# Sliding-window attention in a hybrid decoder layer: one logit per key column, and value sums over block differences

## The chip, the cores and the metric

The kernel runs on one core of a Trainium2 chip. The metric is the device time of one execution in microseconds. The kernel before took 890.16 us (median of three runs, 889.65 to 890.69).

## What is computed

One decoder layer on 512 tokens of width 1024. A shared RMS-normalised input feeds two branches: a chunkwise mLSTM with 4 heads, and sliding-window attention with 16 query heads of width 64, 4 key/value heads and one sink logit per head. The branches are gated, merged and projected, and an MLP, a gated per-layer embedding and a final norm follow. The change lies in the attention alone:

```python
W = SW_WINDOW            # 128, so 4 blocks of queries
kb, vb = band(k), band(v)        # a block's keys: left neighbour's 128, then its own 128
logits = einsum("bnqhgd,bnkhd->bnhgqk", qb, kb) * SW_HEAD_DIM ** -0.5
diff = qi + W - ki
band_mask = (diff >= 0) & (diff < W)
logits = where(valid, logits, -inf)              # block 0 has no left neighbour
m = maximum(max(logits, -1), sink)
pexp = exp(logits - m)
probs = pexp / (sum(pexp, -1) + exp(sink - m))
out = einsum("bnhgqk,bnkhd->bnqhgd", probs, vb)
```

For query row q of a block and column k from 0 to 127, the mask lets through the block's own key k if k <= q, and the left neighbour's key k if k > q. So of the two keys in column k exactly one is valid.

## The kernel before

The layer is one program of five in-order instruction streams (TensorE, VectorE, ScalarE, GpSimd, SyncE), and the framework orders the instructions of each stream from the Python code. Weights arrive in fp32, and nearly every projection is made of three matmuls per product: `split` (L134) lets ScalarE round a tile to a high part (L137, `wh`) and VectorE subtract for the low part (L138, `wl`), and `chain` (L171) multiplies high by high, high by low and low by high. One projection of 512 columns is a chain of 24 matmuls into an accumulator `psg`, of which there are two.

PSUM is shared out in three tags: two `psg` and two `pst` tiles of 128x512, and two `psa` tiles of 128x1024. The attention takes its logits and its transposes from the two `psa` tiles, and the value sums from `pst`.

The attention works in units (kp, n, ab): a pair of key heads, a block n of 128 queries and one key head of the pair, with four query heads `g` each; 16 units in all, 12 of them with n > 0. Two functions carry it.

- `swa_probs` (L683): eight score matmuls (L689 with the high part of the keys, L690 with the low part) fill a `psa` tile with 4 x 256 logits. VectorE's custom instruction (L697, four per unit, 256 columns or 128 for n = 0) scales, adds the mask `band` and takes the row maximum with the sink into `mx`, writing the logits to `lm`. After two small VectorE steps (L701, L703), ScalarE takes four exponentials with row sums (L708), and VectorE normalises (L709, L711, L712).
- `swa_out` (L715), once per pair of units: for each of the two key blocks (`nk`, one for n = 0), TensorE transposes eight 128x128 pieces of `lm` into a `psa` tile (L726) and ScalarE copies it to `pT` (L728). Two matmuls in fp32 per block (L734, two records each in the trace) then sum the values `vs` into a `pst` tile, which four `split` steps turn into `yb`.

The loop (L750) scores two units ahead (`LOOK`) and puts one query or mLSTM projection (`q_proj`, `qk_proj`) between units as filling for TensorE. The masks are built once at the start: `band` on GpSimd (L213 to L216), and `tri` (L217), which is 0 where column >= row and -1e30 elsewhere. At the start GpSimd also rounds the first weights (L327), VectorE subtracts for their low part (L328) and for that of the normalised input (L317).

Of the kernel before, what the change touches and what calls it, by code (L numbers as in the profile page):

```python
# [22 lines left out]
NEG = -1e30  # L23
# [13 lines left out]
def block_kernel(  # L37
# [30 lines left out]
    V, A, G, T = nc.vector, nc.scalar, nc.gpsimd, nc.tensor  # L68
# [12 lines left out]
    c1 = pool(st_s, "c1", side="right")  # L81
    sp = pool(st_s, "sp", side="right")
# [4 lines left out]
    def nm(s):  # L87
        n_names[0] += 1
        return f"{s}_{n_names[0]}"
# [8 lines left out]
    def ps_a():  # L98
        return pp.tile([P, 1024], F32, tag="a", bufs=2, name=nm("psa"))
# [23 lines left out]
    def tok_scratch(n="lm"):  # L123
        return sp.tile([P, D], F32, tag="lm", bufs=LMB, name=nm(n))
# [9 lines left out]
    def split(dst, src, scale=None):  # L134

        if scale is None:
            A.copy(dst[0], src)  # L137
            last_low[0] = V.tensor_sub(dst[1], src, r32(dst[0]))  # L138
        else:
            A.activation(dst[0], src, AF.Copy, scale=scale)  # L140
            V.scalar_tensor_tensor(dst[1], src, scale, r32(dst[0]), ALU.mult, ALU.subtract)
# [60 lines left out]
    ident = cp.tile([P, P], F32, name="ident")  # L202
# [4 lines left out]

    cp.tile([P, 16], F32, name="pad")
    V.memset(eps_t, EPS)
    zeros4 = c1.tile([4, P], F32, name="zeros4")  # L210
    V.memset(zeros4, 0.0)
    band = c1.tile([P, 2 * P], F32, name="band")
    G.memset(band, 0.0)  # L213

    G.affine_select(out=band, in_=band, pattern=[[1, 2 * P]], compare_op=ALU.is_gt, fill=NEG, base=0, channel_multiplier=-1)
    G.affine_select(out=band, in_=band, pattern=[[-1, 2 * P]], compare_op=ALU.is_ge, fill=NEG, base=P, channel_multiplier=1)  # L216
    tri = c1.tile([P, P], F32, name="tri")  # L217
    G.memset(tri, 0.0)

# [36 lines left out]
    sink = c1.tile([P, 16], F32, name="sink")  # L256
# [31 lines left out]
    vs = []  # L288
# [392 lines left out]
    probs = {}  # L681

    def swa_probs(kp, n, ab):  # L683
        k0 = max(n - 1, 0) * P
        ls = ps_a()
        for g in range(4):
            q = qs[kp * 4 + g, ab]
            o = ls[:, g * 256 : (g + 1) * 256]
            T.matmul(o, q[:, n * P : (n + 1) * P], kk[kp][ab][:, k0 : k0 + 256], start=True, stop=False)  # L689
            T.matmul(o, q[:, n * P : (n + 1) * P], kl[kp][ab][:, k0 : k0 + 256], start=False, stop=True)  # L690
        W = P if n == 0 else 2 * P
        kv = 2 * kp + ab
        sk = sink[:, kv * 4 : kv * 4 + 4]
        lm3 = tok_scratch().rearrange("p (g k) -> p g k", g=4)[:, :, :W]
        mx = small("mx", 4)
        for g in range(4):
            V.tensor_tensor_reduce(  # L697
                lm3[:, g, :], ls[:, g * 256 : g * 256 + W], band[:, 256 - W :], 0.125, sk[:, g : g + 1], ALU.add, ALU.max, mx[:, g : g + 1]
            )
        nmx = small("nmx", 4)  # L700
        V.tensor_scalar_mul(nmx, mx, -1.0)  # L701
        ds = small("ds", 4)
        V.tensor_sub(ds, sk, mx)  # L703
        es = small("es", 4)
        A.activation(es, ds, AF.Exp)
        sm = small("sm", 4)
        for g in range(4):
            A.activation(lm3[:, g, :], lm3[:, g, :], AF.Exp, bias=nmx[:, g : g + 1], accum_out=sm[:, g : g + 1])  # L708
        V.tensor_add(sm, sm, es)  # L709
        rc = small("rc", 4)  # L710
        V.reciprocal(rc, sm)  # L711
        V.tensor_tensor(lm3, lm3, rc.unsqueeze(2).broadcast_to([P, 4, W]), ALU.mult)  # L712
        probs[kp, n, ab] = lm3

    def swa_out(kp, n):  # L715


        nk = 1 if n == 0 else 2
        lm3 = [probs.pop((kp, n, ab)) for ab in range(2)]
        pTs = []  # L720
        for j in range(nk):
            pt = ps_a()
            for ab in range(2):
                for g in range(4):
                    c = ab * 512 + g * P
                    T.transpose(pt[:, c : c + P], lm3[ab][:, g, j * P : (j + 1) * P], ident)  # L726
            pT = sp.tile([P, 1024], F32, tag="pT", bufs=2, name=nm("pT"))
            A.copy(pT, pt)  # L728
            pTs.append(pT)
        o = ps_t()  # L730
        for j in range(nk):
            for ab in range(2):
                c = (2 * kp + ab) * 64
                T.matmul(  # L734
                    o[HALF[ab], :],
                    vs[n + 1 - nk + j][:, c : c + 64],
                    pTs[j][:, ab * 512 : (ab + 1) * 512],
                    start=j == 0,
                    stop=j == nk - 1,
                )  # L740
        for g in range(4):
            if n == 0:
                yb[kp * 4 + g] = act_hl("yb")
            split([t[:, n * P : (n + 1) * P] for t in yb[kp * 4 + g]], o[:, g * P : (g + 1) * P])

    fill = [lambda: qk_proj(0)] + [lambda i=i: q_proj(i) for i in range(4, 8)]
    fill += [lambda i=i: qk_proj(i) for i in (4, 1, 5, 2, 6, 3)]
# [668 lines left out]
```

## Time and profile before

| | |
|---|---|
| median of three runs | 890.16 us |
| the profiled execution | 889.58 us |
| its span in the profile | 887.8 us |
| instructions | 11800 |
| TensorE busy | 875.5 us |
| VectorE busy | 663.1 us |
| ScalarE busy | 486.8 us |

The span runs from the first to the last recorded instruction; 1.8 us of the execution lie around it. Engines: PE is TensorE's matmuls, PEld its weight loads, DVE is VectorE, ACT ScalarE, POOL GpSimd. Matmuls are pipelined, so that the time from one start to the next says what one costs, not its own duration. The attention stands between 221 us (first score matmul) and 328 us (last value sum).

### The profile page before, as it was taken

How to read it: one execution, taken by the hardware profiler on the slowest of the kernel's cores; microseconds unless marked ns; L12 is line 12 of the kernel's file. 1: busy time of each engine (PE TensorE's matmuls, PEld its weight loads, DVE VectorE, ACT ScalarE, POOL GpSimd, SP SyncE). 2: the span in 40 equal slices, each digit the busy share in tenths (PEclk: the TensorE clock that was granted, in tenths of full speed). 3: DMA queues.
4: the chain of work that ended last, by engine and by line, in shares of the span. 5: the costliest groups of instructions: out<-in, count | busy, mean ns of one | idle time of the engine just before them, and what ended most of it. 6: DMA issues, size and time to landing. Idle time of an engine off the chain costs nothing.

```text
span 887.8 us, 11800 instructions
## 1 busy us (share of the span) xinstructions
PE 875.5 (99%) x4452; PEld 733.5 (83%) x4452; DVE 663.1 (75%) x1066; ACT 486.8 (55%) x802; POOL 30.3 (3%) x53
## 2 busy tenths in 40 slices
PE   8999999999999999999999999999999999999996
PEld 7888889998877677788888888888888888888886
DVE  6899887874887967575896669746966794689566
ACT  6684554444776758743354565345435534554853
POOL 2111010000000000000020000000000000000000
PEclk9999999999999999999999999999999999999999
DMA  8665144435111053273234611620352054101402
GB/s 278 187 183 186 72 153 171 169 105 188 55 65 64 33 172 115 93 253 125 97 63 132 255 48 48 212 96 25 111 182 87 0 184 148 48 24 50 165 1 95
DMA packets 32363, 105.19 MB, mean 118 GB/s; under 512 B 4525, under 2 KB 5037, under 8 KB 32306
## 3 DMA queue, kind: packets, MB, share of 16 engines
q1 hardware_dynamic: 28002, 93.15, 30.4%
q0 software_dynamic: 4160, 11.02, 4.8%
q8 instruction: 35, 0.57, 0.3%
q10 hardware_dynamic: 144, 0.26, 0.1%
q14 instruction: 22, 0.18, 0.1%
HBM read 91.30 MB, written 8.40 MB: 112 GB/s over the span
## 4 chain that ended last, share of the span: by engine, by line
PE 93%; DVE 3%; ACT 2%; DMA 1%; issue 1%; SPq 0%; ACTq 0%; DVEq 0%
PE psg L171 52%; PE psp L171 22%; PE psa L171 7%; PE pst L171 4%; PE pst L734 1%; PE psa L816 1%; PE psa L726 1%; PE psa L689 1%; PE psa L690 1%; DVE wl L138 1%; PE psa L804 1%; PE psg L263 1%; DMA wr<-in_w_gb 0%; PE pst L858 0%; PE psp L973 0%
## 5 line engine op out<-in xcount | busy, mean ns | idle before, releaser
L137 ACT CAST wh<-wr 128x1024 fp32r<-128x1024 f32 x138 | 144.8, 1052 | 180.7 <-PE psg L171 79.0
L138 DVE TENSOR_TENSOR wl<-wr,wh 128x1024 fp32r<-128x1024 f32 x138 | 167.5, 1219 | 89.3 <-ACT wh L137 89.0
L171 PE MATMUL psg<-x,wh 128*128 128x512 f32 x512 | 157.7, 389 | 0.0
L171 PE MATMUL psp<-wh,uf 128*128 128x512 f32 x448 | 139.2, 390 | 0.0
L171 PEld LDWEIGHTS psg<-x,wh 128*128 128x128 f32 x512 | 96.0, 188 | 19.9
L171 PE MATMUL psg<-x,wl 128*128 128x512 f32 x256 | 99.6, 389 | 0.0
L171 PEld LDWEIGHTS psp<-wh,uf 128*128 128x128 f32 x448 | 84.1, 188 | 17.4
L171 PE MATMUL psp<-wl,uf 128*128 128x512 f32 x224 | 87.2, 390 | 0.0
L171 PE MATMUL psg<-h,wh 128*128 128x512 f32 x256 | 81.4, 396 | 0.0
L137 ACT CAST wh<-wd 128x1024 fp32r<-128x1024 f32 x44 | 46.2, 1053 | 57.3 <-PE psp L171 23.6
L138 DVE TENSOR_TENSOR wl<-wd,wh 128x1024 fp32r<-128x1024 f32 x44 | 53.2, 1218 | 15.8 <-ACT wh L137 15.7
L171 PEld LDWEIGHTS psg<-h,wh 128*128 128x128 f32 x256 | 46.9, 188 | 13.5 <-issue 4.9
L171 PEld LDWEIGHTS psg<-x,wl 128*128 128x128 f32 x256 | 48.1, 188 | 10.0
L171 PE MATMUL psg<-h,wl 128*128 128x512 f32 x128 | 50.3, 393 | 0.0
L138 DVE TENSOR_TENSOR uf<-F,uf 128x1792 fp32r<-128x1792 f32 (+2 forms) x20 | 33.0, 1652 | 21.8 <-ACT uf L137 21.8
L171 PEld LDWEIGHTS psp<-wl,uf 128*128 128x128 f32 x224 | 42.1, 188 | 8.7
L171 PE MATMUL psg<-yb,wh 128*128 128x512 f32 x128 | 41.5, 402 | 0.0
L171 PE MATMUL psg<-ya,wh 128*128 128x512 f32 x128 | 39.5, 390 | 0.0
L137 ACT CAST uf<-F 128x1792 fp32r<-128x1792 f32 (+2 forms) x20 | 27.9, 1396 | 20.5 <-DVE F L1118 20.4
L1142 DVE SCALAR_TENSOR_TENSOR xk<-psp,r,xk 128x512 f32<-128x512 f32 x48 | 33.8, 744 | 3.5 <-PE psp L171 3.2
L171 PE MATMUL psg<-hS,wh 128*128 128x256 f32 x192 | 35.6, 284 | 0.0
L171 PE MATMUL psa<-h,wh 128*128 128x256 f32 x192 | 35.3, 285 | 0.2 <-ACT p L625 0.2
(316 smaller groups left out, 1779.2 us busy)
## 6 DMA issues: line engine op xcount, KB each, us to landing
wr<-in_w_up SPq DMA_DIRECT2D x32, 512.0 KB, 3.3
wd<-in_w_down SPq DMA_DIRECT2D x24, 512.0 KB, 3.4
wr<-in_w_qsw SPq DMA_DIRECT2D x8, 512.0 KB, 4.2
gd<-gr POOLq DMA_DIRECT2D x8, 512.0 KB, 3.0
wr<-in_w_qkml SPq DMA_DIRECT2D x8, 512.0 KB, 3.2
wr<-in_w_b SPq DMA_DIRECT2D x8, 512.0 KB, 3.1
gl<-gd SPq DMA_DIRECT2D x8, 512.0 KB, 3.5
wr<-in_w_a SPq DMA_DIRECT2D x8, 512.0 KB, 4.2
```

Of the source, the lines that this page charges most:

```text
L137: A.copy(dst[0], src)
L138: last_low[0] = V.tensor_sub(dst[1], src, r32(dst[0]))
L171: last_mm[0] = T.matmul(ps, l, r, start=first and i == 0, stop=last and i == len(ops) - 1, skip_group_check=parts)
L263: tc.keep_in_program_order(T.matmul(idle[bank][:, :P], ones, ones, start=True, stop=True))
L689: T.matmul(o, q[:, n * P : (n + 1) * P], kk[kp][ab][:, k0 : k0 + 256], start=True, stop=False)
L690: T.matmul(o, q[:, n * P : (n + 1) * P], kl[kp][ab][:, k0 : k0 + 256], start=False, stop=True)
L726: T.transpose(pt[:, c : c + P], lm3[ab][:, g, j * P : (j + 1) * P], ident)
L734: T.matmul(o[HALF[ab], :], vs[n + 1 - nk + j][:, c : c + 64], pTs[j][:, ab * 512 : (ab + 1) * 512], start=j == 0, stop=j == nk - 1,)
L804: T.matmul(psc, qk[4 + h][:, n0 : n0 + P], qk[h][:, n0:], start=True, stop=True, skip_group_check=True)
L816: last_mm[0] = T.matmul(pn[:, t % 2, : DV + 1], wT[s][:, t * P : (t + 1) * P], vm[s][:, h, :], start=s == 0, stop=s == t, skip_group_check ...
L1142: pin(V.scalar_tensor_tensor(o, ps[:, t, :], r2[:, 2 * toks + t : 2 * toks + t + 1], o, ALU.mult, ALU.add))
```

## The change

Both blocks' scores are computed as before, but of the two logits in a column only the valid one is kept. For n > 0, ScalarE copies the own block's 4 x 128 logits to `lm`, and VectorE overwrites the later columns (mask `later_key`, non-zero where column > row) with the left neighbour's, by a predicated copy from PSUM. For n = 0 one add of the mask does. A plain maximum over 4 x 128 columns follows, and scale and sink come into the next small step through `nsink`, the negated sinks. Exponentials and normalisation run over 128 columns in place of 256, and a pair is transposed once.

The transposed weights `pT` then hold own and left keys mixed. The value sum is taken as (all weights) x (left values) + (own keys' weights) x (own values - left values): `own` is `pT` with the other entries zeroed, one VectorE instruction on 128x1024 out of PSUM, and `vd` are the differences of neighbouring blocks' values, made once (the last one in place of `vs[3]`).

```diff
-    zeros4 = c1.tile([4, P], F32, name="zeros4")
-    V.memset(zeros4, 0.0)
-    band = c1.tile([P, 2 * P], F32, name="band")
-    G.memset(band, 0.0)
-    G.affine_select(out=band, ... pattern=[[1, 2 * P]], compare_op=ALU.is_gt, ...)
-    G.affine_select(out=band, ... pattern=[[-1, 2 * P]], compare_op=ALU.is_ge, ...)
+    zero4 = c1.tile([4, 1], F32, name="zero4")
+    zeros4 = zero4.broadcast_to([4, P])
+    later_key = c1.tile([P, P], F32, name="later_key")
+    G.memset(later_key, 0.0)
+    G.affine_select(out=later_key, ... pattern=[[-1, P]], compare_op=ALU.is_ge, fill=NEG, base=0, channel_multiplier=1)
...
     def swa_probs(kp, n, ab):
-        lm3 = tok_scratch().rearrange("p (g k) -> p g k", g=4)[:, :, :W]
-        for g in range(4):
-            V.tensor_tensor_reduce(
-                lm3[:, g, :], ls[:, g * 256 : g * 256 + W], band[:, 256 - W :], 0.125, sk[:, g : g + 1], ALU.add, ALU.max, mx[:, g : g + 1]
-            )
-        V.tensor_scalar_mul(nmx, mx, -1.0)
-        V.tensor_sub(ds, sk, mx)
+        lm3 = tok_scratch()[:, :512].rearrange("p (g k) -> p g k", g=4)
+        if n == 0:
+            V.tensor_tensor(lm3, ls3[:, :, :P], later_key.unsqueeze(1).broadcast_to([P, 4, P]), ALU.add)
+        else:
+            A.copy(lm3, ls3[:, :, P:])
+            V.copy_predicated(lm3, later_key.bitcast(mybir.dt.int32).unsqueeze(1).broadcast_to([P, 4, P]), ls3[:, :, :P])
+        V.tensor_reduce(mx, lm3, AX.X, ALU.max, negate=True)
+        V.scalar_tensor_tensor(nmx, mx, 0.125, nsink[:, kv * 4 : kv * 4 + 4], ALU.mult, ALU.min)
+        V.tensor_add(ds, sk, nmx)
...
     def swa_out(kp, n):
-        for j in range(nk):
-            pt = ps_a()
-            ...eight transposes of lm3[ab][:, g, j * P : (j + 1) * P]...
-            A.copy(pT, pt)
+        pt = ps_a()
+        ...eight transposes of lm3[ab][:, g, :]...
+        A.copy(pT, pt)
+        terms = [(vs[max(n - 1, 0)], pT)]
+        if n:
+            own = sp.tile([P, 1024], F32, tag="pT", bufs=2, name=nm("pT"))
+            V.scalar_tensor_tensor(own, tri (eight times over), 0.0, pt, ALU.is_ge, ALU.mult)
+            terms.insert(0, (vd[n], own))
-                T.matmul(o[HALF[ab], :], vs[n + 1 - nk + j][:, c : c + 64], pTs[j][:, ab * 512 : (ab + 1) * 512], ...)
+                T.matmul(o[HALF[ab], :], v[:, c : c + 64], w[:, ab * 512 : (ab + 1) * 512], ...)
...
+    V.tensor_scalar_mul(nsink, sink, -1.0)
+    for n in (3, 2, 1):
+        V.tensor_sub(vd[n], vs[n], vs[n - 1])
```

The framework orders the new instructions anew from here to the end of the attention, and a few at the program's start. Three places follow.

TensorE, where the second pair of units (`lm_2352` and its neighbour) is transposed. Before (L726 transposes, L734 the value sum, L171 a projection's matmuls):

```order
L726 MATMUL psa_2567<-ident,lm_2352 128x128 x4
L726 MATMUL psa_2567<-ident,lm_2419 128x128 x4
L171 MATMUL psg_2602<-h_161,wl_2606 128x512
L171 MATMUL psg_2602<-h_161,wh_2605 128x512
L171 MATMUL psg_2602<-h_162,wh_2605 128x512
L171 MATMUL psg_2602<-h_161,wl_2606 128x512
L726 MATMUL psa_2578<-ident,lm_2352 128x128 x4
L726 MATMUL psa_2578<-ident,lm_2419 128x128 x4
```

Now (`psa_2534` are the logits scored just ahead; L689 and L690 are the scores):

```order
L689 MATMUL psa_2534<-kk_439,qs_2241 128x256
L690 MATMUL psa_2534<-kl_441,qs_2241 128x256
L171 MATMUL psg_2589<-h_158,wh_2592 128x512
L171 MATMUL psg_2589<-h_159,wh_2592 128x512
L171 MATMUL psg_2589<-h_158,wl_2593 128x512
L171 MATMUL psg_2589<-h_158,wh_2592 128x512
L171 MATMUL psg_2589<-h_159,wh_2592 128x512
L171 MATMUL psg_2589<-h_158,wl_2593 128x512
L726 MATMUL psa_2563<-ident,lm_2352 128x128 x4
L726 MATMUL psa_2563<-ident,lm_2418 128x128 x4
```

The second eight transposes are gone, and the one group that is left stands six projection matmuls behind the scores, where the first group stood seventeen behind them; eleven projection matmuls later all four value matmuls follow in one place.

VectorE at the same place, from the normalisation of the second pair's last unit on. Before (L697 ISA is the custom logit instruction, and its second row the read of its maximum):

```order
L712 TENSOR_TENSOR lm_2419<-lm_2419,rc_2437 128x1024
L138 TENSOR_TENSOR yb_2467<-pst_2451,yb_2466 128x128
L697 ISA lm_2516,mx_2517<-psa_2507,band,sink 128x256
L697 ISA mx_2517 128x1
L425 TENSOR_TENSOR qs_2501<-psg_2470,qs_2501 64x512
```

Now (L701 the predicated copy, L734 the masking into `own`, L716 the normalisation; lines of the changed kernel):

```order
L716 TENSOR_TENSOR lm_2418<-lm_2418,rc_2435 128x512
L138 TENSOR_TENSOR wl_2869<-wr_2866,wh_2868 128x1024
L138 TENSOR_TENSOR yb_2461<-pst_2449,yb_2460 128x128
L701 COPY_PREDICATED lm_2514<-later_key,psa_2505 128x512
L138 TENSOR_TENSOR yb_2465<-pst_2449,yb_2464 128x128
L703 TENSOR_REDUCE mx_2517<-lm_2514 128x4
L425 TENSOR_TENSOR qs_2499<-psg_2468,qs_2499 64x512
L705 SCALAR_TENSOR_TENSOR nmx_2519<-mx_2517,nsink 128x4
L701 COPY_PREDICATED lm_2543<-later_key,psa_2534 128x512
L707 TENSOR_TENSOR ds_2521<-sink,nmx_2519 128x4
L734 SCALAR_TENSOR_TENSOR pT_2574<-tri,psa_2563 128x1024
```

A weight's low part (`wl_2869`) and a `yb` step now stand between the normalisation and the predicated copy that empties `psa_2505`, and the masking stands behind a second predicated copy.

VectorE at the program's start. Before (L328 is the first weights' low part, L317 the input's):

```order
L300 SCALAR_TENSOR_TENSOR xn_163<-xt_105,rs_168,psa_138 128x512
L317 TENSOR_TENSOR h_162<-pst_176,h_161 128x4x128
L328 TENSOR_TENSOR wl_173<-wr_113,wh_172 128x792
L317 TENSOR_TENSOR h_162<-pst_177,h_161 128x4x128
L285 RECIPROCAL rs_195<-sd_193 128x1
```

Now:

```order
L300 SCALAR_TENSOR_TENSOR xn_160<-xt_102,rs_165,psa_135 128x512
L328 TENSOR_TENSOR wl_170<-wr_110,wh_169 128x792
L317 TENSOR_TENSOR h_159<-pst_173,h_158 128x4x128
L317 TENSOR_TENSOR h_159<-pst_174,h_158 128x4x128
L285 RECIPROCAL rs_192<-sd_190 128x1
```

The weights' low part moves ahead of the input's; `nsink` and the three `vd` come some twenty to forty rows later on the same engine, among the first projections.

More of the change, by code (lines that the diff above doesn't have):

```diff
@@ L707, in swa_probs @@
         for g in range(4):
-            A.activation(lm3[:, g, :], lm3[:, g, :], AF.Exp, bias=nmx[:, g : g + 1], accum_out=sm[:, g : g + 1])
+            A.activation(lm3[:, g, :], lm3[:, g, :], AF.Exp, bias=nmx[:, g : g + 1], scale=0.125, accum_out=sm[:, g : g + 1])
         V.tensor_add(sm, sm, es)
@@ L744, in swa_out @@
             split([t[:, n * P : (n + 1) * P] for t in yb[kp * 4 + g]], o[:, g * P : (g + 1) * P])
+    nsink = c1.tile([P, 16], F32, name="nsink")
+    V.tensor_scalar_mul(nsink, sink, -1.0)
+    vd = [None] + [sp.tile([P, 256], F32, tag="vd", bufs=2, name=nm("vd")) for _ in range(2)] + [vs[3]]
+    for n in (3, 2, 1):
+        V.tensor_sub(vd[n], vs[n], vs[n - 1])
     fill = [lambda: qk_proj(0)] + [lambda i=i: q_proj(i) for i in range(4, 8)]
```

39 lines of the change are left out of this document (19 added, 20 removed).

## The prediction

> **What bounds the kernel now.** I read the page's busy times and its chain of waits first, then the busy times of the attention's stretch, the groups of instructions by form, the waits of that stretch, and the timeline around its transposes.
>
> The page's busy times and the shares of the chain that ended last:
>
> ```profile
> PE 875.5 (99%) x4452; PEld 733.5 (83%) x4452; DVE 663.1 (75%) x1066; ACT 486.8 (55%) x802; POOL 30.3 (3%) x53
> PE 93%; DVE 3%; ACT 2%; DMA 1%; issue 1%; SPq 0%; ACTq 0%; DVEq 0%
> ```
>
> TensorE carries 93% of the chain. What it need not do is time gained, if nothing else then ends last. Whether that holds in the attention itself is read from the stretch from 220 to 335 us (columns: stretch, length, busy time and count of PE, PEld, DVE, ACT and POOL, granted clock, DMA share, GB/s):
>
> ```profile
> 220.00:335.00 115.00, 113.16 (x598) 85.75 (x597) 89.96 (x285) 76.86 (x222) 0.00 (x0) 1.00 0.25 85
> ```
>
> There too PE is busy for 113.2 of 115 us, at a granted clock of 1.00. VectorE has 90.0 us of work in it and ScalarE 76.9: both are within a fifth to a third of the bound, so that a late one can be felt, but neither sets the pace. DMA is at 0.25 and plays no part.
>
> **The change part by part.** First the terms, from the groups by form (busy us, mean ns of one, idle before and releaser):
>
> ```profile
> L726 PE MATMUL psa<-ident,lm 128*128 128x128 f32 x112 | 14.4, 273 | 1.6 <-ACT pT L728 1.6
> L734 PE MATMUL pst<-pT,vs 128*64 128x512 f32 x56 | 14.9, 618 | 0.2
> L697 DVE CUSTOM_DVE_ANT_0 lm<-psa,band,sink 128x256 f32<-128x256 f32 x48 | 21.6, 477 | 6.5 <-PE psa L690 6.4
> L697 DVE CUSTOM_DVE_ANT_0 lm<-psa,band,sink 128x128 f32<-128x128 f32 x16 | 4.8, 343 | 1.9 <-PE psa L690 1.8
> L712 DVE TENSOR_TENSOR lm<-lm,rc 128x1024 f32<-128x1024 f32 x12 | 14.7, 1222 | 0.2
> L712 DVE TENSOR_TENSOR lm<-lm,rc 128x512 f32<-128x512 f32 x4 | 2.7, 687 | 0.1
> L708 ACT ACTIVATE lm<-lm,nmx 128x256 f32<-128x256 f32 x48 | 23.8, 498 | 7.9 <-DVE nmx L701 5.8 <-DVE ds L703 2.1
> L708 ACT ACTIVATE lm<-lm,nmx 128x128 f32<-128x128 f32 x16 | 6.2, 391 | 1.1 <-DVE nmx L701 1.1
> L728 ACT COPY pT<-psa 128x1024 f32<-128x1024 f32 x14 | 14.0, 1011 | 5.2 <-PE psa L726 5.2
> L888 DVE TENSOR_TENSOR sga<-psg,gl 128x512 f32<-128x512 f32 x8 | 5.5, 688 | 8.3 <-PE psg L171 8.3
> L138 DVE TENSOR_TENSOR wl<-wr,wh 128x1024 fp32r<-128x1024 f32 x138 | 167.5, 1219 | 89.3 <-ACT wh L137 89.0
> L507 ACT COPY p<-pst x4: 587/587/589, 49.7 to 90.3; 128x512 f32<-128x512 f32 x4
> ```
>
> And the start times of TensorE at two pairs of transposes (start, duration, what; the first three rows are one place, the rest another):
>
> ```profile
> 236.22 1.04 PE L726 MATMUL psa<-ident,lm 128*128 128x128 f32 x8
> 237.02 0.71 PE L171 MATMUL psg<-h,wh 128*128 128x512 f32 x2
> ...
> 299.79 0.39 PE L171 MATMUL psg<-h,wl 128*128 128x512 f32 x1
> 300.02 0.28 PE L689 MATMUL psa<-kk,qs 128*128 128x256 f32 x1
> 300.13 0.28 PE L690 MATMUL psa<-kl,qs 128*128 128x256 f32 x1
> ...
> 300.97 1.04 PE L726 MATMUL psa<-ident,lm 128*128 128x128 f32 x8
> 303.61 1.09 PE L726 MATMUL psa<-ident,lm 128*128 128x128 f32 x8 [1.60 <-ACT pT L728]
> ```
>
> *TensorE, removed.* For n > 0 there are six pairs of units (three blocks, two key pairs), and each loses one of its two groups of eight transposes: 48 of 112. Eight of them take 237.02 - 236.22 = 0.80 us from start to start, 0.100 each; the group's busy time by its count, 14.4 / 112 = 0.129, holds some of the waiting around them and is the other end. So 4.8 to 6.2 us; I take 4.8, since start to start is what the next matmul sees. The value matmuls stay 28 (56 records, since the n > 0 pairs have two terms before and after), and all 128 score matmuls stay, both blocks being scored as before.
>
> The Trainium skill (TensorE: Matmul & The Clock Gate, section "Back-to-back issue gap") gives a sustained stream of load and matmul pairs at N = 128 about 81 ns each; by that the 48 would be an estimated 3.9 us and the forecast 0.9 us later. The trace's 100 ns decides here.
>
> *TensorE, a wait that goes.* The second group needs its own `psa` tile, and with only two of them it can wait for the copy of the first. At 300.97 eight transposes start, and the next eight start 2.64 us later, where 0.80 would do: 1.84 us, of which the profile puts 1.60 down to the copy L728. With one group per pair this goes; I take the 1.6. The stretch's other waits of this kind:
>
> ```profile
> PEld pst L734 <- ACT pT L728: 3.1, 6, 1.0
> PE psa L726 <- ACT pT L728: 1.6, 1, 1.6
> ```
>
> *Value sums.* Before, six waited 3.1 us in all for a copy `pT` (1.011 us on ScalarE). Now the first two value matmuls of a pair wait for `own`, one pass of 128x1024 out of PSUM on VectorE. The trace has that pass only for SBUF (L138, 1.219); I take 1.22. It starts with the ScalarE copy rather than after it, but on the busier engine, behind whatever stands there. Against it, more projection matmuls now stand between transposes and sum (eleven at the place shown). Bounds: all 3.1 us saved, or 1.22 us at each of the six, 7.3 us, which is 4.2 more than before. I take no change, 0.
>
> *VectorE.* Removed: the L697 passes, 21.6 + 4.8 = 26.4 us, and twelve normalisations that halve, 12 x (1.222 - 0.687) = 6.4. Added: twelve predicated copies, sixteen maxima and four mask adds, each over 128x512 and priced at the nearest rows (L888 out of PSUM 0.688, L712 from SBUF 0.687): 32 x 0.69 = 22.1; six `own`, 7.3. Removed 32.8, added 29.4: 3.4 us less, leaving some 86.6 us in the stretch. The small steps (`nmx`, `ds`) exchange one for one. A predicated copy and a maximum of this form are in no row; the lower end is the custom pass per element (477 ns for 256, so 0.95 us for 512 is the upper one of that kind, and 0.343 for one pass of 128 the lower), which makes 28 of them 9.6 to 26.6 us against my 19.3. All of it lies beside TensorE's work as long as VectorE's sum stays below the stretch.
>
> The Trainium skill (VectorE: DVE Perf Modes, section "Rules for kernel authors") advises against `tensor_reduce` on a hot path as VectorE's slowest operation, at one element per cycle. No row here shows one; by that rule the sixteen new ones are the part of the change to watch, and the slower case below is where it would lead.
>
> *ScalarE.* Removed: 48 x (0.498 - 0.391) = 5.1, and six `pT` copies, 6.1. Added: twelve copies of 128x512 out of PSUM at 0.587 (L507): 7.0. Net 4.2 us less, all beside TensorE.
>
> *A wait that comes.* A unit's logits now leave their `psa` tile in two steps on two engines, the copy and then the predicated copy, and the program's order puts the transposes closer behind. At the second pair (the order shown), the transposes go into the tile that `psa_2505` held. Between the end of its scores and them, TensorE has eight score matmuls at 0.11 and six of a projection at 0.23 (the rows from 299.79 on): 0.9 + 1.4 = 2.3 us. The predicated copy stands behind the normalisation of `lm_2418`, which the same transposes read, then a `wl` (1.22) and a `yb` step (about 0.3, as an estimate between the 0.687 of 512 columns and the small steps), and takes 0.69 itself: 2.2 us from the moment at which the transposes could otherwise start. If VectorE is ahead by then it costs nothing, else up to 2.2. I take 1.2, the middle, since the unit's exponentials on ScalarE stand behind `yb` casts that wait for the value sum before. Queued behind the waiting transposes is TensorE's whole stream; nothing overtakes it. Elsewhere the order leaves four or more microseconds between scores and the next use of their tile, except at one pair of units (2.4 us), where no `wl` stands in between.
>
> *The program's start.* TensorE and VectorE there:
>
> ```profile
> 9.77 0.56 PE L171 MATMUL psg<-wh,h 128*128 128x264 f32 x1
> 11.64 0.59 PE L171 MATMUL psg<-wl,h 128*128 128x264 f32 x1 [1.31 <-DVE wl L328]
> 9.66 0.69 DVE L317 TENSOR_TENSOR h<-pst,h 128x512 fp32r<-128x512 f32 x1 [1.64 <-ACT h L316]
> 10.27 1.32 DVE L328 TENSOR_TENSOR wl<-wr,wh 128x792 fp32r<-128x792 f32 x1
> ```
>
> `wl` now comes ahead of `h`, into VectorE's idle 1.64 us, and the wait of 1.31 us goes. What is late next are the second token block's transposes, which need its norm; that chain is untouched, so most of it comes back as another wait. The three `vd` (128x256 each, between a small step and 0.69; about 0.4 as an estimate) and `nsink` add some 1.3 us to VectorE while TensorE has weights ahead. Bounds -1.3 and +1.3; I take 0. GpSimd's shorter mask work is idle time there anyway.
>
> **The sum.** -4.8 - 1.6 + 0 + 1.2 + 0 = -5.2 us. After the attention, TensorE is the bound to the end, and loads are issued as tiles come free, so they move along. The profiled execution took 889.58 us, its span 887.8; 889.58 - 5.2 = 884.4. The median is 0.58 above that execution, so 885.0.
>
> **The rivals.** What a measurement can tell from no change is about 0.2%, 1.8 us.
>
> 1. *The waits go as well (20%).* The transposes at 0.100, the 1.6, most of the 3.1 of the value sums and part of the start's 1.3, with no new wait: 4.8 + 1.6 + 2 + 0.5 = 8.9, so 881.3. For it: the value sums now stand further from their transposes. Against: VectorE at 90 of 115 us has its queue rarely empty, and `own` stands behind other steps.
>
> 2. *Half is given back (13%).* TensorE waits at about half the six value sums for `own` and at the second pair in full: 4.8 + 1.6 - 3 x 1.2 - 1.2 = 1.6, so 888.5, just within what can't be told from no change. For it: at several pairs VectorE has convolution steps of `acc` and a `wl` ahead of `own`.
>
> 3. *Slower: the two-step release of the logits' tile (12%).* Each of the twelve units' tiles is free only after a ScalarE step and a VectorE step, each in an in-order queue. A ScalarE weight cast ahead is a further microsecond, a `wl` ahead 1.219. If on average 1.0 us of that reaches TensorE at the twelve units, 12.0 - 6.4 = 5.6 us are lost: 895.8. It decides from 6.4 / 12 = 0.53 us per unit. Dearer predicated copies and maxima (0.95 each instead of 0.69) add to it, 7.3 us of VectorE time, though VectorE's sum would still be below the stretch. Against it: today's wait for these tiles is small,
>
> ```profile
> PEld psa L689 <- DVE mx L697: 0.8, 1, 0.8
> DVE lm L697 <- PE psa L690: 8.2, 7, 2.1
> ```
>
> 0.8 us once, with 1.9 us of VectorE passes per unit ahead of a tile's release (four of 0.477), where 0.587 + 0.69 stand now; and VectorE waits ten times as long for the scores as TensorE for VectorE.
>
> That the change does not take the work away is excluded by the order, which has 64 transposes where 112 stood. My forecast proper has 55%.
>
> **How the numbers follow.** The likeliest case gives 885.0. Its own range comes from 6.2 in place of 4.8 below, and the full 2.2 of the new wait with 1 us of value-sum waits above: 883.5 to 887. The range that should hold the time 8 times in 10 reaches to the first rival below and half a microsecond past the second above: 881.3 to 889.0. The forecast and the first rival are faster by over 0.2%, and so is about a third of the second: 80%. The rest of the second, 8%, is within 0.2%; the third, 12%, is slower.
>
> **What would show it.** 64 transposes at L726 with a start-to-start of 0.10 us; no `[... <-ACT pT]` ahead of a group of transposes; the predicated copies and maxima near 0.69 us; value sums waiting for `pT` of line 734 at 3 us or less in all; VectorE near 87 us in the stretch; the first score matmul still at 221 us, and all of the gain between it and the first mLSTM score. Wrong would be: a second line of waits of TensorE on the predicated copy above 6 us in all, a VectorE busy for more than 105 us of the stretch, or a gain that is there at the attention's end and gone at the program's.

## The result, and the profile after

The changed kernel takes **882.21 us** (median of four runs, 881.84 to 882.56) against 890.1 us (889.65 to 890.69): 7.9 us less, a ratio of 0.9912 with a 95% interval from 0.9900 to 0.9923. The forecast was 885.0 us in a range from 881.3 to 889.0: the direction was right and the time lies in the range, but the gain is half as large again as the forecast 5.2 us. The profiled execution took 882.08 us, with a span of 880.3.

The page's busy times of the changed kernel:

```profile
PE 868.6 (99%) x4404; PEld 727.8 (83%) x4404; DVE 662.1 (75%) x980; ACT 481.8 (55%) x808; POOL 28.9 (3%) x52
```

TensorE has 48 instructions less and is busy for 6.9 us less; VectorE hardly changed. The same stretch from 220 to 335 us as before (stretch, length, PE, PEld, DVE, ACT, POOL, granted clock, DMA share, GB/s), and a shorter one that ends where the mLSTM has not begun:

```profile
220.00:335.00 115.00, 113.58 (x578) 85.82 (x577) 95.55 (x205) 80.06 (x239) 0.00 (x0) 1.00 0.27 88
220.00:330.00 110.00, 108.72 (x559) 82.47 (x557) 90.55 (x196) 75.08 (x231) 0.00 (x0) 1.00 0.28 90
```

TensorE stays the bound at a clock of 1.00. VectorE's 95.6 us are not the 86.6 of the prediction. In good part that is later work that has moved into the stretch: between 330 and 335 us VectorE is busy for 5.0 us now, and was for 0.9. In the shorter one the kernel before had this:

```profile
220.00:330.00 110.00, 108.16 (x576) 81.63 (x575) 89.04 (x282) 74.91 (x218) 0.00 (x0) 1.00 0.22 74
```

TensorE was idle for 110 - 108.16 = 1.84 us of it, and is for 1.28 now.

The instructions of three lines say where the gain lies (count, least, median and largest ns, first and last start). Before:

```profile
L689 PE MATMUL psa<-kk,qs x64: 277/283/387, 221.2 to 314.1; 128*128 128x256 f32 x64
L804 PE MATMUL psa<-acc,acc x24: 272/486/697, 339.3 to 376.3; 128*128 128x512 f32 x8, 128*128 128x384 f32 x8, 128*128 128x128 f32 x8
L171 PE MATMUL psg<-x,wh x512: 389/389/477, 491.3 to 781.0; 128*128 128x512 f32 x171
```

After:

```profile
L689 PE MATMUL psa<-kk,qs x64: 277/283/387, 220.1 to 308.2; 128*128 128x256 f32 x64
L819 PE MATMUL psa<-acc,acc x24: 272/486/697, 332.1 to 368.3; 128*128 128x512 f32 x8, 128*128 128x384 f32 x8, 128*128 128x128 f32 x8
L171 PE MATMUL psg<-x,wh x512: 389/389/477, 483.4 to 773.1; 128*128 128x512 f32 x171
```

The first score matmul comes 1.1 us earlier (221.2 to 220.1), so some of the gain was made before the attention. The first mLSTM score comes 7.2 us earlier (339.3 to 332.1), with three more projection matmuls already done ahead of it (0.68 us), so at equal work the lead is 7.9. Of that, 7.9 - 1.1 = 6.8 us belong to the attention. The lead then stays: the first matmul of the up-projection moved from 491.3 to 483.4 us, 7.9 again.

What made the 6.8 us is read by adding up TensorE's rows between these two points, each from its start to the next start, without idle time. The transposes take 7.3 us where they took 12.2, the value sums 13.1 for 14.0, the scores 15.09 for 15.95; the projections take 0.3 more, the three extra matmuls not counted, and idle time fell from 1.84 to 1.42 (to 1.28 up to 330 us). So 4.9 of the 6.8 us are the transposes, 0.9 each the value sums and the scores, and 0.4 idle time. The value sums have as many rows as before, two for each fp32 matmul, but stand in eight places instead of twelve. Before, four rows in a row hold the stream for 239.38 - 238.37 = 1.01 us:

```profile
238.37 1.08 PE L734 MATMUL pst<-pT,vs 128*64 128x512 f32 x4
239.38 0.50 PE L171 MATMUL psg<-h,wl 128*128 128x512 f32 x1
```

After, eight rows in a row take 251.71 - 249.84 = 1.87, less than twice that:

```profile
249.84 1.08 PE L747 MATMUL pst<-pT,vd 128*64 128x512 f32 x4
...
251.71 0.50 PE L171 MATMUL psg<-h,wl 128*128 128x512 f32 x1
```

Why the scores stand closer was not followed.

The new and the changed instructions in the groups by form of the changed kernel (busy, mean ns of one, idle before):

```profile
L726 PE MATMUL psa<-ident,lm 128*128 128x128 f32 x64 | 8.7, 273 | 0.0
L703 DVE TENSOR_REDUCE mx<-lm 128x4 f32<-128x512 f32 x16 | 10.8, 681 | 0.1
L701 DVE COPY_PREDICATED lm<-later_key,psa 128x512 f32<-128x512 int32 x12 | 8.7, 732 | 0.0
L734 DVE SCALAR_TENSOR_TENSOR pT<-tri,psa 128x1024 f32<-128x1024 f32 x6 | 7.3, 1212 | 0.0
L696 DVE TENSOR_TENSOR lm<-psa,later_key 128x512 f32<-128x512 f32 x4 | 2.8, 689 | 0.8 <-PE psa L690 0.6
L700 ACT COPY lm<-psa 128x512 f32<-128x512 f32 x12 | 7.0, 584 | 4.4 <-PE psa L690 4.4
```

Each price of the prediction held within 7%: the predicated copy 0.732 us against 0.69, the maximum 0.681 against 0.69, the masking 1.212 against 1.22, the copy 0.584 against 0.587. The Trainium skill (VectorE: DVE Perf Modes, section "Rules for kernel authors") advises against `tensor_reduce` as VectorE's slowest operation; here it costs no more than the mask add of the same size (0.689).

TensorE's waits between 215 and 340 us (waiting tile and line, releaser: us in total, times, longest), PE for the matmuls' own waits, PEld for those of the weight loads; some of the attention's, among them every wait of PE above 0.2 us:

```profile
PEld pst L747 <- ACT pT L728: 1.0, 2, 0.6
PEld psa L689 <- DVE lm L701: 0.9, 1, 0.9
PE psg L171 <- DVE rc L715: 0.6, 1, 0.6
PE psa L689 <- DVE lm L701: 0.5, 1, 0.5
PEld pst L747 <- DVE pT L734: 0.4, 1, 0.4
PEld psa L726 <- DVE lm L701: 0.2, 1, 0.2
```

No group of transposes waits for a copy any more. The value sums' weight loads wait 1.0 + 0.4 us for `pT` where they waited 3.1; most of that lay beside running matmuls, since the value matmuls themselves idled for only 0.2 us both before and after. The new wait for the predicated copy exists: at one score the load waits 0.9 us and the matmul 0.5. A projection waits 0.6 us for VectorE, which the kernel before did not have either. At the transposes the load waits 0.2 us, and the matmuls do not wait. There, at the second pair (start, duration, what):

```profile
246.13 0.39 PE L171 MATMUL psg<-h,wl 128*128 128x512 f32 x1
246.36 1.04 PE L726 MATMUL psa<-ident,lm 128*128 128x128 f32 x8
247.16 0.71 PE L171 MATMUL psg<-h,wh 128*128 128x512 f32 x2
...
245.50 0.73 DVE L701 COPY_PREDICATED lm<-later_key,psa 128x512 f32<-128x512 int32 x1
```

The predicated copy ends at 246.23 us, 0.10 after the last projection matmul has started. The transposes follow that matmul at its own spacing of 0.23 us, so the forecast 1.2 us did not come at this place. Eight of them take 247.16 - 246.36 = 0.80 us, as before.

### The profile page after: what moved, and what is told of

The parts are those of the page before. It is cut to its first block, busy times and chain, and to the rows that moved or that the text cites. A ratio compares the mean times of both kernels' runs of the same rounds, so it can differ in the third digit from the quotient of the medians.

```text
span 880.3 us, 11620 instructions
## 1 busy us (share of the span) xinstructions
PE 868.6 (99%) x4404; PEld 727.8 (83%) x4404; DVE 662.1 (75%) x980; ACT 481.8 (55%) x808; POOL 28.9 (3%) x52
## 4 chain that ended last, share of the span: by engine, by line
PE 75%; DVE 3%; ACT 3%; issue 1%; DMA 0%; SPq 0%; ACTq 0%
PE psg L171 43%; PE psp L171 22%; PE psa L171 4%; PE psa L831 1%; PE pst L747 1%; DVE wl L138 1%; ACT lm L712 1%; PE psa L819 1%; ACT wh L137 1%; PE psa L689 1%; PE psa L690 1%; PE psa L726 0%; PE pst L873 0%; PE psp L988 0%; DVE qs L425 0%
## 5 line engine op out<-in xcount | busy, mean ns | idle before, releaser
L171 PE MATMUL psg<-x,wh 128*128 128x512 f32 x512 | 157.7, 389 | 0.0
L171 PE MATMUL psp<-wh,uf 128*128 128x512 f32 x448 | 139.2, 390 | 0.0
L171 PEld LDWEIGHTS psg<-x,wh 128*128 128x128 f32 x512 | 96.0, 188 | 19.8
L171 PE MATMUL psg<-x,wl 128*128 128x512 f32 x256 | 99.6, 389 | 0.0
L171 PEld LDWEIGHTS psp<-wh,uf 128*128 128x128 f32 x448 | 84.1, 188 | 17.4
L171 PE MATMUL psp<-wl,uf 128*128 128x512 f32 x224 | 87.2, 390 | 0.0
L171 PE MATMUL psg<-h,wh 128*128 128x512 f32 x256 | 81.0, 395 | 0.6 <-DVE rc L715 0.6
L171 PEld LDWEIGHTS psg<-x,wl 128*128 128x128 f32 x256 | 48.0, 188 | 10.1
L171 PEld LDWEIGHTS psg<-h,wh 128*128 128x128 f32 x256 | 47.0, 188 | 11.2 <-issue 1.6
L171 PE MATMUL psg<-h,wl 128*128 128x512 f32 x128 | 50.5, 395 | 0.0
L171 PEld LDWEIGHTS psp<-wl,uf 128*128 128x128 f32 x224 | 42.0, 188 | 8.7
L171 PE MATMUL psg<-yb,wh 128*128 128x512 f32 x128 | 41.3, 402 | 0.1
L171 PE MATMUL psg<-ya,wh 128*128 128x512 f32 x128 | 39.5, 390 | 0.0
L171 PE MATMUL psg<-hS,wh 128*128 128x256 f32 x192 | 35.6, 284 | 0.0
L171 PE MATMUL psa<-h,wh 128*128 128x256 f32 x192 | 35.3, 285 | 0.3 <-ACT p L625 0.2
```

Of the source, the lines that this page charges most:

```text
L171: last_mm[0] = T.matmul(ps, l, r, start=first and i == 0, stop=last and i == len(ops) - 1, skip_group_check=parts)
```

## The experiments

The edits are made to the changed kernel, except in the second of the two runs on the start. Times are medians; all kernels ran beside the kernel before, at 889.9 to 890.0 us (890.9 beside the last one, a single execution).

**What a transpose costs.** Each of the 48 transposes of n > 0 is done twice into the same tile.

```diff
                 T.transpose(pt[:, c : c + P], lm3[ab][:, g, :], ident)
+                if n:
+                    T.transpose(pt[:, c : c + P], lm3[ab][:, g, :], ident)
```

> The changed kernel with each of the 48 transposes of the six pairs with n > 0 done twice into the same tile (same data, no further tile, no further copy). If a transpose costs TensorE its 0.100 us from start to start: 4.8 us slower than the changed kernel, 887.0. Rival, that the gain lay in waits and the transposes were mostly covered by waits around them: under 2.5 us slower, below 884.7. A sustained 81 ns each, as the Trainium skill has it (TensorE: Matmul & The Clock Gate, section Back-to-back issue gap), would give 886.1.

Measured: 886.55 us (886.07 to 887.31), ratio 0.9963 (0.9950 to 0.9975): 4.3 us more than the changed kernel, 0.090 for each transpose. The medians agree with the term of 4.8 to half a microsecond; the ranges of the runs leave 3.5 to 5.5. It can't carry the whole 7.9.

**The second tile and its copy.** A second group of eight goes into a `psa` tile of its own, and ScalarE copies that too, as before the change.

```diff
         A.copy(pT, pt)
+        if n:
+            pt2 = ps_a()
+            ...the eight transposes again, into pt2...
+            A.copy(pT, pt2)
```

> The changed kernel with the second group of eight transposes of a pair put back as it stood before: into a tile of its own, copied by ScalarE over the same weights. Work as in twice_T (4.8 us), plus the wait for a free tile: 1.6 us and more of the value sums' waits if these were part of the gain, so 888.6 to 889.5. Rival, that the tile was no part of the gain: as twice_T, 887.0.

Measured: 887.32 us (886.99 to 887.96), ratio 0.9972 (0.9962 to 0.9982). That is 0.8 more than with the transposes alone, in intervals that overlap, and less than expected. Its waits, the second tile being L734 and L735:

```profile
PEld pst L754 <- ACT pT L735: 1.2, 2, 0.8
PEld psa L734 <- DVE lm L701: 0.9, 1, 0.9
PEld psa L689 <- ACT pT L735: 0.9, 2, 0.4
```

The 1.6 us wait did not return as one; the order is another one, and the tile is waited for in smaller pieces. So the tile's price is not settled: 0.8 us here, 1.6 in the trace of before.

**The start, from both sides.** First the changed kernel with GpSimd's mask instruction done three times, which brings VectorE's old order at the start back:

```diff
     G.affine_select(out=later_key, ... channel_multiplier=1)
+    G.affine_select(out=later_key, ... channel_multiplier=1)
+    G.affine_select(out=later_key, ... channel_multiplier=1)
```

> The changed kernel with the first mask built three times over on GpSimd (same values), which puts the first weights' low part on VectorE back behind the input's, as before the change; the attention's order is untouched. If the 1.1 us by which the first score matmul came earlier is the start's reorder: 1.1 us slower than the changed kernel, 883.3, with the 1.3 us wait of TensorE for the weights' low part back. Rival, that the earlier start comes from something else or is given back later: no change, 882.2.

Measured: 882.72 us (881.64 to 884.21), ratio 0.9921 (0.9907 to 0.9934), 0.5 more in a wide spread, which decides nothing. The wait came back, and yet the first score started at 220.3 us, only 0.2 later than in the changed kernel. First matmuls of the start in this kernel, and the line of its first and last score:

```profile
9.78 0.36 PE L171 MATMUL psg<-wh,h 128*128 128x264 f32 x1
...
11.30 0.39 PE L171 MATMUL psg<-wl,h 128*128 128x264 f32 x1 [1.17 <-DVE wl L330]
...
L691 PE MATMUL psa<-kk,qs x64: 277/283/387, 220.3 to 308.4; 128*128 128x256 f32 x64
```

In the changed kernel the wait for the low part is gone, but the second token block's transposes (L311) and the matmul behind them wait for 0.91 and 0.24 us:

```profile
9.77 0.56 PE L171 MATMUL psg<-wh,h 128*128 128x264 f32 x1
...
12.98 1.22 PE L311 MATMUL psa<-ident,xn 128*128 128x128 f32 x8 [0.91 <-ACT xn L296]
14.45 0.39 PE L171 MATMUL psg<-wl,h 128*128 128x264 f32 x1 [0.24 <-DVE wl L328]
```

In the kernel before, the same transposes came without a wait of their own, but later: the projection ahead of them stood behind the 1.31 us wait and then ran at a slower pace:

```profile
13.35 0.64 PE L171 MATMUL psg<-wh,h 128*128 128x264 f32 x2
13.79 1.55 PE L311 MATMUL psa<-ident,xn 128*128 128x128 f32 x8
15.09 0.37 PE L171 MATMUL psg<-wl,h 128*128 128x264 f32 x1
```

There two matmuls of 264 columns take 13.79 - 13.35 = 0.44 us, and from 15.3 us on some 0.25. With the masks tripled they take 0.24 from 11.53 on, and the same transposes start at 12.85. So the traces' 1.1 us holds both the order and the pace of the first matmuls, and the pace differs between these executions.

Then the kernel before, with its masks built behind the first weights' casts, which gives VectorE the start of the changed kernel and changes nothing else:

```diff
-    G.memset(band, 0.0)
-    ...the three G.affine_select of band and tri, and G.memset(tri, 0.0)...
...
+    G.memset(band, 0.0)
+    ...the same four, behind the first weights' casts...
     def proj_T(wd, i, bank=ps_g):
```

> The kernel before, with its masks built on GpSimd behind the first weights: this alone puts VectorE's order at the start as in the changed kernel (the weights' low part first); the attention's order is as before. If the start's reorder is worth the 1.1 us by which the first score came earlier: 1.1 us faster than the kernel before, 888.8 to 889.1. Rival, that the earlier start was the matmul clock's phase at the program's start, which differs from run to run: no difference between the medians, and a profile whose first score moves with the pace of the first matmuls and not with the order.

Measured: 888.74 us (888.13 to 889.65, 11 runs) against 889.97 (15 runs), ratio 0.9986 (0.9977 to 0.9995). By the medians the reorder at the start is worth 1.2 us by itself, between 0.4 and 2.0. The profile does not show where: its first score comes only 0.3 us ahead of the kernel before (221.2), behind a start in which the granted clock is near 0.50 from 13 to 16 us:

```profile
L691 PE MATMUL psa<-kk,qs x64: 277/283/388, 220.9 to 313.8; 128*128 128x256 f32 x64
```

So the first score moves with the pace in the profiles, as the rival had it, while the medians differ, which the rival excludes. Two causes would fit both: the new order leaves its wait of 0.91 us as slack when the pace is slow, or the faster pace comes with it more often. No run tells them apart.

**Old softmax, new value sums.** The logits of both blocks go through the old custom instruction and exponentials over 256 columns; one add joins the two halves before a normalisation over 128. One group of transposes and the new value sums stay; the masks, and with them the start's order, are those of before; a constant row of the start also takes its tile from another pool.

```diff
-        A.copy(lm3, ls3[:, :, P:]); V.copy_predicated(...); V.tensor_reduce(...)
+        ...four V.tensor_tensor_reduce(...), as before, over 256 columns...
+        if n:
+            V.tensor_add(lm3[:, :, :P], lm3[:, :, :P], lm3[:, :, P:])
```

> Half of the change: the softmax as before over both blocks (custom logit pass and exponentials over 256 columns), then one add of the two blocks' weights per unit, normalisation over 128 columns, and the value sums as changed. TensorE's work is that of the changed kernel, VectorE has some 12.6 us more in the attention, and the program's start is in the order of before. If the gain is TensorE's transposes: 1.1 us from the start plus up to 2 us of waits, 883.3 to 885.5. Rival, that the lighter softmax made the gain: 887 and above.

Measured: 886.69 us (886.58 to 887.59), ratio 0.9965 (0.9951 to 0.9978), 4.5 more than the changed kernel, between the two expectations and close to the rival's 887. The start's old order may hold 1.2 of it. One place in the attention stands out, in its timeline and its windows:

```profile
302.85 1.19 PE L171 MATMUL psg<-h,wh 128*128 128x512 f32 x2 [4.38 <-DVE acc L668]
...
303.00:308.00 5.00, 5.00 (x16) 3.50 (x18) 4.23 (x10) 1.87 (x8) 0.00 (x0) 0.50 0.01 3
...
220.00:330.00 110.00, 105.53 (x537) 81.11 (x536) 94.94 (x298) 69.28 (x211) 0.00 (x0) 0.97 0.24 79
```

TensorE waits once for 4.38 us, for a VectorE convolution step, and then runs at half its clock for five microseconds more, some 2.5 us of work. Together that is more than the whole loss; where the rest was won back was not followed. The profiled execution took 887.59 us; all five list a mean granted clock of 0.993 to 0.997, where the changed kernel's list 0.996 to 0.999. VectorE has 94.9 us of 110 here. Was it VectorE's sum, or that one place?

**VectorE's sum.** The masking `own` is done twice: 6 x 1.21 = 7.3 us more on VectorE, at a place that the value sums wait for.

```diff
             V.scalar_tensor_tensor(own, tri, 0.0, pt, ALU.is_ge, ALU.mult)
+            V.scalar_tensor_tensor(own, tri, 0.0, pt, ALU.is_ge, ALU.mult)
```

> The changed kernel with the masking into own done twice (same values): 7.3 us more VectorE work in the attention, none for TensorE. If VectorE is close to setting the pace, as the half change suggested, TensorE's waits on VectorE grow: 884 to 886. Rival, that VectorE lies beside TensorE's work with room to spare and the half change lost only to its own order: under 0.7 us slower, below 882.9.

Measured: 882.59 us (882.46 to 883.04), ratio 0.9916 (0.9902 to 0.9929), 0.4 more: the rival's number.

```profile
220.00:330.00 110.00, 108.77 (x556) 82.09 (x555) 96.05 (x202) 76.65 (x234) 0.00 (x0) 1.00 0.26 83
```

VectorE now carries 96.05 of 110 us, more than in the experiment before it, and TensorE is as busy as in the changed kernel (108.77 against 108.72). So VectorE's sum does not set the time here. That the place of a single step does is what the 4.38 us wait of the experiment before suggests.

**The predicated copy twice.** 12 x 0.73 = 8.8 us more on VectorE, now between the scores and the release of their tile.

```diff
             V.copy_predicated(lm3, later_key, ls3[:, :, :P])
+            V.copy_predicated(lm3, later_key, ls3[:, :, :P])
```

> The changed kernel with the predicated copy done twice (same values): each of the twelve units with n > 0 holds its logits' tile 0.73 us longer, and VectorE has 8.8 us more. If the two-step release of the tile reaches TensorE (the slower rival of the prediction): up to 12 x 0.73 = 8.8 us slower, and at least 4, so 886 to 891. If the tile is nearly always free in time, as TensorE's 1.6 us of waits on the predicated copy say: under 1.5 us slower, 882.3 to 883.7.

Measured: 885.25 us (883.27 to 887.51), ratio 0.9947 (0.9935 to 0.9958), 3.0 more, between the expectations. The trace shows one new wait, and the same kernel was profiled a second time:

> The kernel with the predicated copy done twice, profiled once more: its runs lay between 883.3 and 887.5, and the profiled one was the fastest, with one wait of TensorE of 3.3 us and a granted clock of 1.00 throughout. If the spread comes from the clock dropping to half behind that wait in some executions: a time near 885 or above, with a stretch of some 3 to 6 us at 0.5 behind the wait. If the waits themselves vary: a time off 883.3 with the clock at 1.00 and longer waits.

It took 884.83 us; the first profiled execution took 883.27. Timeline and windows of the first:

```profile
301.07 0.70 PE L171 MATMUL psg<-h,wh 128*128 128x512 f32 x2 [3.31 <-DVE sm L714]
...
301.00:303.00 2.00, 1.93 (x9) 1.62 (x10) 2.00 (x5) 0.00 (x0) 0.00 (x0) 1.00 0.00 0
303.00:305.00 2.00, 2.00 (x11) 1.68 (x10) 2.00 (x3) 0.00 (x0) 0.00 (x0) 1.00 0.00 0
```

And of the second:

```profile
301.05 0.70 PE L171 MATMUL psg<-h,wh 128*128 128x512 f32 x2 [3.31 <-DVE sm L714]
...
301.00:303.00 2.00, 1.95 (x6) 1.61 (x7) 2.00 (x5) 0.00 (x0) 0.00 (x0) 0.66 0.01 2
303.00:305.00 2.00, 2.00 (x7) 1.51 (x6) 2.00 (x3) 0.00 (x0) 0.00 (x0) 0.50 0.00 0
```

The third column from the end is the granted clock. Up to the wait the two agree to 0.02 us (301.07 and 301.05), and the wait is 3.31 us in both. Behind it the clock is 1.00 in one and falls to 0.66 and 0.50 in the other, which loses 2 x 0.34 + 2 x 0.50 = 1.7 us; the executions differ by 1.56. The other five timed executions list a mean clock of 0.994 to 0.997 and 884.5 to 887.5 us, the first 0.999, so the fall is the common case. The wait itself costs less than its length: with it, TensorE is idle for 110 - 106.66 = 3.34 us from 220 to 330 us, against 1.28, since the smaller waits are gone, and the first execution is only 1.2 us slower than the profiled one of the changed kernel (882.08).

**Scores of n = 0 over 128 columns.** The left half of those scores is never read.

```diff
-            T.matmul(o, q[...], kk[kp][ab][:, k0 : k0 + 256], start=True, stop=False)
+            kw = 256 if n else P
+            T.matmul(o, q[...], kk[kp][ab][:, k0 : k0 + kw], start=True, stop=False)
             ...kl likewise...
```

> The changed kernel with the first block's scores taken over the 128 columns that exist, instead of 256: 32 score matmuls of half the width. If a matmul's place in the stream goes by its columns: 32 x 0.06 = 1.9 us faster than the changed kernel, 880.3. If the weight load sets the pace, as for the transposes of 128 columns at 0.100: 32 x 0.015 = 0.5, 881.7.

Measured: 883.2 us (882.62 to 885.17), ratio 0.9927 (0.9915 to 0.9939), 1.0 slower and a miss. Start to start, a score of 128 columns takes 0.112 us, one of 256 takes 0.120 (medians), so 32 of them save 0.3 us. And the new order puts a score ahead of its query. Timeline and windows:

```profile
223.87 0.33 PE L690 MATMUL psa<-kk,qs 128*128 128x128 f32 x1 [1.35 <-DVE qs L425]
...
224.00:225.00 1.00, 1.00 (x5) 0.83 (x6) 0.54 (x1) 0.98 (x2) 0.00 (x0) 0.87 0.73 229
225.00:226.00 1.00, 1.00 (x5) 0.79 (x4) 0.94 (x3) 0.73 (x1) 0.00 (x0) 0.50 0.74 295
226.00:227.00 1.00, 1.00 (x3) 0.81 (x3) 1.00 (x2) 0.00 (x0) 0.00 (x0) 0.50 0.06 16
```

A wait of 1.35 us, and behind it some three microseconds at half the clock, ate more than was saved in this execution (885.17 us, mean clock 0.994). Three others, at 882.6 to 883.2 us, list a mean clock of 0.998, so the clock can have fallen little there, and the waits are the likelier cause: besides the 1.35 us, the value matmuls idle for 1.2 us for the masking.

**Scores three units ahead.** The logits of a pair's two units share one scratch tile (each fills half of it since the change), which leaves room to score three units ahead instead of two.

```diff
-LOOK = 2
+LOOK = 3
...
-        lm3 = tok_scratch()[:, :512]...
+        if ab == 0:
+            pair_lm[kp, n] = tok_scratch()
+        lm3 = pair_lm[kp, n][:, ab * 512 : (ab + 1) * 512]...
```

> The changed kernel with the scores three units ahead instead of two, both units of a pair sharing one scratch tile. If what is left of TensorE's waits in the attention (some 3 us at named places) comes from the distance between scores and use: 1 to 2 us faster, 880.5 to 881.2. Rival, that the two accumulator tiles set the distance: no change, or slower where scores wait for a tile.

Measured: 880.55 us (880.12 to 881.06), ratio 0.9894 (0.9879 to 0.9909), the fastest median; every run of it is below every run of the changed kernel, though the intervals of the two ratios overlap.

```profile
220.00:330.00 110.00, 109.56 (x562) 83.30 (x561) 91.87 (x199) 75.93 (x234) 0.00 (x0) 1.00 0.28 91
```

TensorE is idle for 0.44 of the 110 us, where it was for 1.28. As a control, the shared tile with `LOOK = 2`:

> The control for the kernel with scores three units ahead: both units of a pair share one scratch tile, and the scores stay two ahead. If the distance between scores and use made the 1.7 us: as the changed kernel, 882.2. If the sharing did (more scratch tiles free for what follows): 880.6.

Measured: 881.63 us (881.43 to 881.83), ratio 0.9906 (0.9891 to 0.9920). Some 0.6 us come with the shared tile and 1.1 with the distance, by medians; the intervals overlap.

Both ideas together, the third unit ahead and the narrow scores:

> The first block's scores over 128 columns and the scores three units ahead. The narrow scores alone were a microsecond slower, with TensorE waiting 4 us for the masking into own at places where the order had moved. If these waits came from that order and go with the longer distance: 880.0, half a microsecond below the three-ahead kernel. If the narrow scores cost something themselves (their load no longer covered): above 881.

Measured: 885.65 us (884.05 to 886.84), ratio 0.9951 (0.9939 to 0.9962), 5.1 slower than the first alone. The same score stands ahead of its query, with the same 1.35 us and the half clock behind it (the profiled execution took 886.84 us; all five list a mean clock of 0.994 to 0.997). The 4 us named in the expectation add the weight loads' 3.0 us to the matmuls' own 1.2, though the two overlap.

```profile
223.87 0.33 PE L691 MATMUL psa<-kk,qs 128*128 128x128 f32 x1 [1.35 <-DVE qs L425]
...
226.00:228.00 2.00, 2.00 (x10) 1.90 (x10) 1.99 (x5) 0.00 (x0) 0.00 (x0) 0.50 0.03 8
```

## Why the prediction was right, and by how much it was not

- **Transposes, -4.8: right.** 64 stand where 112 stood, at 0.100 us from start to start; doing 48 again cost 4.3, and the trace's rows add up to 4.9 less. The estimate of 3.9 from the Trainium skill (TensorE: Matmul & The Clock Gate, section "Back-to-back issue gap") lies 0.4 below the run, the trace's row 0.5 above it.
- **The tile wait, -1.6: gone from the trace**, though bringing a second tile back cost only 0.8 beyond its transposes.
- **Value sums, 0: mis-sized.** The prediction looked at their waits alone, and rightly expected little: the value matmuls idled for 0.2 us before and after. But the eight rows of a pair now stand together, and TensorE's own time for the value sums fell by 0.9 us.
- **The new wait, +1.2: right in its sum by luck.** At the second pair it did not come: VectorE had emptied at 246.23 us the tile that the transposes fill from 246.36 on, 0.13 us ahead. But a score now waits 0.5 us for a predicated copy and a projection 0.6 us for VectorE, at two places that the prediction did not name. So idle time fell by 0.4 us, as -1.6 + 1.2 had it.
- **The start, 0: mis-sized.** That most of the wait "comes back as another wait" is what the changed kernel's trace shows: 1.31 us went, 0.91 and 0.24 came. Yet the first score stands at 220.1 us, not still at 221. Moving the masks alone gave 1.2 us (0.4 to 2.0); how much of the traces' 1.1 is the order and how much the pace of that execution stays open.

The gain was missed by 2.7 us. By the traces 1.1 of it lies at the start, 0.9 in the value sums, 0.9 in the scores and 0.1 in the transposes, less 0.3 in the projections; the prediction put its terms for the first two at nothing and counted the scores as unchanged. Rival 1 (the waits go as well, 881.3) has a number nearer to the result than the forecast, but not the mechanism, as new waits did come. Rivals 2 and 3 fell: `own` and the two-step release are waited for in tenths of a microsecond, with the masking done twice the loss was 0.4, and with the predicated copy done twice 3.0. Of the "wrong would be" signs none appeared. VectorE's busy time fell by 1.0 us over the whole program (663.1 to 662.1) where the terms gave 3.4 less 1.3 at the start, 2.1; that had no consequence.

By runs, the start's 1.2, the transposes' 4.3 and the tile with its copy at 0.8 make 6.3 of the 7.9 us; the value sums' and the scores' share is shown by the traces alone. Nor do the parts simply add: with the old softmax put back, the attention's order brought a wait of 4.38 us, and only 3.2 us of the gain were left. Whether some executions of the kernel before also lose clock behind their 1.6 us wait stays open: its one profile shows 1.00 there, and its timed executions list mean clocks of 0.995 to 0.999, much as the changed kernel's do.

## What to carry to other kernels

Price work on the bound engine from start to start, also work that only moves: the same value matmuls cost less in one place than in two. Price a new wait by whether its releaser is ahead in the timeline of before, place by place. Look at the program's start too: a few mask instructions less on an idle engine reordered another engine, and that was worth 1.2 us by the medians, which the diff doesn't show. Before a profile's earlier start is put down to the order, compare the pace of its first matmuls. A small saving that makes the framework order anew (0.3 us for narrower scores) can lose more at one badly placed instruction, so read the new order for a matmul that stands ahead of what it reads.

## What the runs showed of the hardware

A wait of TensorE can cost more than its length. Behind 1.35 us (scores of 128 columns) the granted clock was 0.50 for some three microseconds, and behind 4.38 us (old softmax) for five; behind the same 3.31 us it fell in one execution and not in another, a difference of 1.56 us. At the program's start, waits of 1.33 and 1.35 us ahead of the second token block's transposes left it at 1.00 (masking twice; shared tile with `LOOK = 2`), while in the run with late masks it was near 0.50 from 13 to 16 us behind 1.32. The Trainium skill (TensorE: Matmul & The Clock Gate, section "What's actually happening") tells of half rate after an idle window of about 3.4 us, on a window that runs freely; half rate and its coming in some executions only agree with that, but here it also followed idle times of 1.32 and 1.35 us, well short of such a window.

A score matmul of 128 columns costs nearly what one of 256 does, 0.112 against 0.120 us from start to start: halving its columns saved 7%.

Four rows of fp32 value matmuls together held TensorE's stream for 1.01 us up to the projection behind them, eight for 1.87.
